# The slots' gates in an expert layer: fp32 products, or float32r products with the gates' high and low parts side by side

## Chip, cores and metric

The kernel runs on one core of one Trainium2 chip. The metric is device microseconds of one execution; lower is better. The profiled execution is one further run, whose trace gives the durations used below.

## What is computed

A model of three blocks is applied to 256 tokens of width 1024. Two blocks each end in a two-level mixture of experts; the third has none. For each token, one of four expert groups is picked, and in it two of four experts; each chosen expert's result is weighted by a gate, and all other gates of the token are zero:

```python
gates = sum(one_hot(flat_idx, 16) * (g_w * e_w)[..., None], axis=1)
for e in range(16):
    hid = silu(xt @ w_gate[e]) * (xt @ w_up[e])
    y = y + gates[:, e:e + 1] * (hid @ w_down[e])
```

All arrays are float32. The change lies in how the kernel brings these gates to the place where the experts use them.

## The kernel before

**Work and staging.** 128 partitions hold 128 tokens each of two token tiles, t = 0 and 1. All large weights come from HBM in pieces of 1 MB, by one queue (SP, line 210), into a ring of buffers; in an expert layer there are 17 of them (12 of the kernel's own, 4 and 1 opened for the layer). A new piece is loaded when the buffer that it needs has been freed, so the loads run ahead of TensorE (PE) by up to the size of the ring. An expert takes six pieces: gate and up weights in four, down weights in two.

**An expert layer** (function moe, called at lines 1192 and 1374) routes first, then runs 16 experts in order. Each expert has 64 slots. Which token sits in which slot is held as a one-hot matrix: places(g) (line 770) builds, for the four experts of group g, the tile oh, with tokens on partitions and 4 x 64 slots along the row, in float32r. VectorE (DVE) writes it. PE uses oh to gather the experts' tokens (line 783) as float32r products: the normalised tokens lie there as a high part th and a low part tl, and each is multiplied by oh.

**Gates.** route_done (lines 745 to 762) works out the gates on DVE and ScalarE (ACT); its last instruction writes the tile gates, 128 x 2 x 16 float32. It runs once a layer. slot_gates(g, oh) then carries them from tokens to slots. Four PE products (two pairs of experts i, two token tiles t) have 128 columns of oh, read as float32, as their stationary operand, and four columns of gates as the moving one, accumulating over t into pg, 128 x 8 in PSUM (line 797). DVE multiplies pg by the mask par, which keeps for each half of the partitions the column of its own expert (line 799, tile gs), and sums along the row into gc (line 800). gc is the scalar by which hidden multiplies an expert's hidden values (line 829).

**Where slot_gates stands.** For group 0 it is issued between the gate and up products of expert 0 (lines 817, 818) and its hidden values; right after route_done was issued. For the other three groups it stands at the end of experts 3, 7 and 11: after the down products (line 843) and after gated (lines 850 to 854, which make the tile Y on DVE and ACT), ahead of the gate and up products of the next expert and of scatter (line 860), which adds Y to the tokens' sums z. That is four calls a layer, eight in all.

**Order of the work.** Up to the zeroing and filling of z (lines 960 to 965) the order on PE, DVE and ACT is as written (manual_schedule with three engines). Afterwards only PE's order is as written; the order on DVE and ACT is set when the program is built, by estimated times. Between two experts stands a branch (line 920, more), for experts with more than 64 tokens; values_load reads the count that it tests. The hidden values are transposed (turn, line 836) behind that branch.

Of the kernel before, what the change touches and what calls it, by code (L numbers as in the profile page):

```python
# [10 lines left out]
F32 = mybir.dt.float32  # L11
F32R = mybir.dt.float32r
# [3 lines left out]
OP = mybir.AluOpType  # L16
AX = mybir.AxisListType
# [3 lines left out]
P = 128  # L21
# [151 lines left out]
def model(ctx: ExitStack, tc: tile.TileContext, A, out, stop=None):  # L173
    nc = tc.nc
    V, S, T, G = nc.vector, nc.scalar, nc.tensor, nc.gpsimd
# [5 lines left out]
    def bank(tag, name, shape=(P, 512), dt=F32):  # L181
        return ps.tile(list(shape), dt, name=name, tag=tag)
# [106 lines left out]
    par = cst.tile([P, 2, 4], F32, name="par")  # L289
# [356 lines left out]
    def moe(l, wr, lb, pl, late):  # L646
        a2, b2 = mod[f"a2_{l}"], mod[f"b2_{l}"]
        with more_ring, tc.tile_pool(name=f"moe{l}", bufs=1, reuse_waits="tile") as mp, \
# [6 lines left out]
            sm = lambda shape, n, dt=F32: mp.tile([P] + shape, dt, name=n)  # L655
# [85 lines left out]
            gc = sm([8], "gc")  # L741
            gates = sm([2, 16], "gates")

            def route_done():
                V.tensor_tensor(eg, lg[:, :, 0:4], gm[:, :, None].to_broadcast([P, 2, 4]), op=OP.subtract)
                S.activation(eg, eg, AF.Exp)
                de = sm([2, 4], "de")
                V.tensor_tensor(de, mm2, m1, op=OP.subtract)
                V.tensor_tensor(de, de, og, op=OP.mult)
                V.tensor_reduce(ew[:, 1], de, axis=AX.X, op=OP.add)  # L750
                S.activation(ew[:, 1], ew[:, 1], AF.Exp)
                V.tensor_reduce(gw, eg, axis=AX.X, op=OP.add)
                V.reciprocal(gw, gw)
                V.tensor_scalar(ew[:, 0], ew[:, 1], 1.0, None, op0=OP.add)
                V.reciprocal(ew[:, 0], ew[:, 0])
                V.tensor_tensor(ew[:, 0], ew[:, 0], gw, op=OP.mult)
                V.tensor_tensor(ew[:, 1], ew[:, 1], ew[:, 0], op=OP.mult)
                wide = lambda v: v[..., None].to_broadcast([P, 2, 4, 4])
                for i, o in enumerate((o1, o2)):
                    V.tensor_tensor(de, og, ew[:, i, :, None].to_broadcast([P, 2, 4]), op=OP.mult)  # L760
                    V.tensor_tensor(o, o, wide(de), op=OP.mult)
                V.tensor_tensor(grid(gates), o1, o2, op=OP.add)

            xi = sm([16], "xi", I32)

            def places(g):

                oh = mw.tile([P, 2, 4, 64], F32R, name="oh", bufs=1)
                for t in range(2):
                    V.tensor_tensor(oh[:, t], iota64[:, None, :].to_broadcast([P, 4, 64]),  # L770
                                    r[:, t, 4 * g:4 * g + 4, None].to_broadcast([P, 4, 64]), op=OP.is_equal)
                return oh
# [18 lines left out]

            def slot_gates(g, oh):

                pg = bank("B", "pg")[:, :8].rearrange("p (i e) -> p i e", i=2)
                for i in range(2):
                    for t in range(2):
                        T.matmul(pg[:, i], oh[:, t, 2 * i:2 * i + 2].bitcast(F32), gates[:, t, 4 * g:4 * g + 4], start=t == 0, stop=t == 1)
                gs = mw.tile([P, 2, 4], F32, name="gs")
                V.tensor_tensor(gs, pg, par, op=OP.mult)
                V.tensor_reduce(gc[:, 2 * g:2 * g + 2], gs, axis=AX.X, op=OP.add)  # L800

            def oht_of(e, off):
                p = bank("B", "oht")[:, :256]
# [134 lines left out]
            oh = places(0)  # L938
# [8 lines left out]
            for k in (0, 4):  # L947
                gather(oh, xg, range(k, k + 4), True)
                some_fill(99 if k else FD)
                warm(W[5 + k // 4])  # L950
            route_done()
            nv = nc.values_load(xi[0:1, 0:1], min_val=0, max_val=3)
            tc.mark_branch_hint_location(f"more{l}_0", hint=nv > 0, engines=[mybir.EngineType.PE])
            w = [take(f"moe{l}", 0, t) for t in range(6)]
            hd0 = half(0, w, xg, 0, lambda: slot_gates(0, oh))
            z = [[bank("C", "z"), bank("C", "z")], [bank("D", "z"), bank("D", "z")]]

# [10 lines left out]
            for e in range(16):  # L968
                more(e, w, nv)
                with ExitStack() as part:  # L970
# [22 lines left out]
                    if e in GA:  # L993

                        ks = GA[e]
                        if ks[0] == 0:
                            oh = places(e // 4 + 1)
# [29 lines left out]
                    if e % 4 == 3:  # L1027
                        xg = xn
                        slot_gates(e // 4 + 1, oh)
# [18 lines left out]
    with tc.tile_pool(name="act0", bufs=1, reuse_waits="tile") as pools["act"], \  # L1048
# [71 lines left out]
        oh = pools["act"].tile([P, KD, NT], F32R, name="xh", tag="xh")  # L1120
# [67 lines left out]
    if stop == "xa0":  # L1188
        for t in range(2):
            nc.sync.dma_start(out[t * P:(t + 1) * P], x[t])  # L1190
        return
    sq = moe(0, *rt, pl, ("ada1", "bsh1_1", "bsc1_1", "n1_1", mod["a1_1"], mod["b1_1"]))
    if stop == "xm0":
        for t in range(2):
# [8 lines left out]
    with tc.tile_pool(name="a1", bufs=1, reuse_waits="tile") as a1, tc.tile_pool(name="act1", bufs=1, reuse_waits="tile") as pools["act"], \  # L1203
# [75 lines left out]
        oh = pools["act"].tile([P, KD, NT], F32R, name="oh", tag="xh")  # L1279
# [89 lines left out]
    if stop == "xa1":  # L1369
        for t in range(2):  # L1370
            nc.sync.dma_start(out[t * P:(t + 1) * P], x[t])
        return
    use_c(1)
    sq = moe(1, *rt, pl, ("ada2", "bsh_2", "bsc_2", "gpre", mod["a_2"], mod["b_2"]))
    if stop == "xm1":
        for t in range(2):
# [5 lines left out]
    with tc.tile_pool(name="b2", bufs=1, reuse_waits="tile") as b2, tc.tile_pool(name="act2", bufs=2, reuse_waits="tile") as pools["act"], tc.tile_pool(name="lk2", bufs=2, reuse_waits="tile") as pools["lk"], \  # L1382
# [207 lines left out]
        oh = pools["act"].tile([P, KD, NT], F32R, name="xh", tag="xh")  # L1590
# [19 lines left out]
        p = [bank("A", "pt0"), bank("A", "pt1")]  # L1610
# [35 lines left out]
```

## Time and profile before

| | |
|---|---|
| median of 3 runs | 1191.7 us (1190.25, 1191.7, 1200.09) |
| profiled execution | 1196.26 us, span 1194.4 us |
| PE busy | 1103.3 us, 92% |
| PE weight loads busy | 787.8 us, 66% |
| DVE busy | 644.3 us, 54% |
| ACT busy | 415.2 us, 35% |
| bytes read from HBM | 350 MB, 294 GB/s over the span |

The span runs from the first to the last instruction of the profiled execution; its time has another 1.9 us around it. PE is the matmul itself, PEld the load of the stationary operand, which may lie beside matmuls. One float32 product appears as two records, two weight loads and two matmuls; a float32r product as one of each. The trace writes float32r operands of a product as f32. Busy times of pipelined matmuls overlap, so a pace is read from the starts of a run of them.

### The profile page before, as it was taken

How to read it: one execution, taken by the hardware profiler on the slowest of the kernel's cores; microseconds unless marked ns; L12 is line 12 of the kernel's file. 1: busy time of each engine (PE TensorE's matmuls, PEld its weight loads, DVE VectorE, ACT ScalarE, POOL GpSimd, SP SyncE). 2: the span in 40 equal slices, each digit the busy share in tenths (PEclk: the TensorE clock that was granted, in tenths of full speed). 3: DMA queues.
4: the chain of work that ended last, by engine and by line, in shares of the span. 5: the costliest groups of instructions: out<-in, count | busy, mean ns of one | idle time of the engine just before them, and what ended most of it. 6: DMA issues, size and time to landing. Idle time of an engine off the chain costs nothing. (4 is left out here: it accounts for less than half of the span.)

```text
span 1194.4 us, 20819 instructions
## 1 busy us (share of the span) xinstructions
PE 1103.3 (92%) x8172; PEld 787.8 (66%) x8172; DVE 644.3 (54%) x1488; ACT 415.2 (35%) x802; POOL 23.1 (2%) x48
## 2 busy tenths in 40 slices
PE   5899998999999989999998998998889999999996
PEld 3786565555555469867654554554478889788995
DVE  4665564333333359887632333332399897667566
ACT  2434432111111154365311211111257546455443
POOL 0000000000000000000000000000012000000000
PEclk9899989999999999999999999999999999999998
DMA  9999868999999987668857999998466445543440
GB/s 381 406 396 418 333 232 340 416 415 416 418 417 418 396 311 291 241 227 324 343 218 281 406 407 393 381 406 317 170 212 217 156 148 181 177 165 140 146 172 36
DMA packets 51064, 354.42 MB, mean 297 GB/s; under 512 B 6160, under 2 KB 6544, under 8 KB 9296
## 3 DMA queue, kind: packets, MB, share of 16 engines
q1 hardware_dynamic: 48544, 344.59, 73.7%
q0 software_dynamic: 2064, 7.08, 1.9%
q8 instruction: 104, 1.70, 0.6%
q14 instruction: 64, 0.52, 0.1%
q10 hardware_dynamic: 288, 0.52, 0.1%
HBM read 350.07 MB, written 1.05 MB: 294 GB/s over the span
## 5 line engine op out<-in xcount | busy, mean ns | idle before, releaser
L818 PE MATMUL gu<-ring,xg 128*64 128x256 f32 x1024 | 240.6, 389 | 2.3 <-issue 2.3
L817 PE MATMUL gu<-ring,xg 128*64 128x256 f32 x1024 | 240.3, 389 | 1.9 <-issue 1.8
L473 PE MATMUL pw<-xh,wh 128*128 128x256 f32 x736 | 211.5, 289 | 7.5 <-ACT wh L456 2.6
L459 DVE TENSOR_TENSOR wl<-ring,wh 128x1024 fp32r<-128x1024 f32 x144 | 175.2, 1221 | 74.3 <-ACT wh L456 70.2
L475 PE MATMUL pw<-xh,wl 128*128 128x256 f32 x736 | 209.2, 285 | 0.8 <-DVE wl L459 0.8
L474 PE MATMUL pw<-xl,wh 128*128 128x256 f32 x736 | 208.6, 284 | 0.0
L817 PEld LDWEIGHTS gu<-ring,xg 128*64 128x64 f32 x1024 | 139.6, 140 | 70.5 <-issue 11.2
L456 ACT ACTIVATE wh<-ring 128x1024 fp32r<-128x1024 f32 x114 | 120.0, 1058 | 152.4 <-PE pw L474 75.6
L473 PEld LDWEIGHTS pw<-xh,wh 128*128 128x128 f32 x736 | 141.3, 193 | 19.1 <-issue 10.0
L818 PEld LDWEIGHTS gu<-ring,xg 128*64 128x64 f32 x1024 | 139.6, 140 | 18.9 <-issue 10.4
L475 PEld LDWEIGHTS pw<-xh,wl 128*128 128x128 f32 x736 | 141.6, 193 | 3.5 <-DVE wl L459 1.9
L474 PEld LDWEIGHTS pw<-xl,wh 128*128 128x128 f32 x736 | 141.7, 193 | 0.9 <-DVE ge L1084 0.4
L843 PE MATMUL y<-ring,ht 128*64 128x512 f32 (+1 forms) x576 | 128.3, 563 | 6.7 <-DVE ht L837 5.0
L829 DVE SCALAR_TENSOR_TENSOR hd<-hs,gc,gu 64x256 f32<-64x256 f32 x64 | 30.7, 480 | 165.8 <-ACT hs L828 165.8
L828 ACT ACTIVATE hs<-gu 64x256 f32<-64x256 f32 x66 | 25.0, 378 | 252.1 <-PE gu L818 252.1
L353 PE MATMUL ada<-ring,zc 128*32 128x256 f32 x960 | 68.9, 393 | 14.0 <-DMA ring<-ada 11.3
L843 PEld LDWEIGHTS y<-ring,ht 128*64 128x64 f32 x576 | 39.4, 137 | 53.6 <-issue 33.8
L853 ACT ACTIVATE Y<-yf 64x512 fp32r<-64x512 f32 (+1 forms) x72 | 42.7, 593 | 91.3 <-DVE yf L850 90.4
L854 DVE TENSOR_TENSOR Y<-yf,Y 64x512 fp32r<-64x512 f32 (+1 forms) x72 | 46.2, 642 | 22.7 <-ACT Y L853 21.3
L490 PE MATMUL pt<-wh,xh 128*128 128x512 f32 x144 | 57.0, 398 | 1.0 <-ACT wh L456 0.4
L492 PE MATMUL pt<-wl,xh 128*128 128x512 f32 x144 | 56.5, 392 | 0.5 <-DVE wl L459 0.5
L491 PE MATMUL pt<-wh,xl 128*128 128x512 f32 x144 | 56.3, 391 | 0.0
(391 smaller groups left out, 1528.0 us busy)
## 6 DMA issues: line engine op xcount, KB each, us to landing
ring<-moe SPq DMA_DIRECT2D x192, 1024.0 KB, 9.5
ring<-ada SPq DMA_DIRECT2D x60, 1024.0 KB, 9.5
ring<-b_z SPq DMA_DIRECT2D x24, 1024.0 KB, 4.8
ring<-b_x SPq DMA_DIRECT2D x12, 1024.0 KB, 5.5
ring<-od_q SPq DMA_DIRECT2D x8, 1024.0 KB, 10.1
ring<-ev_q SPq DMA_DIRECT2D x6, 1024.0 KB, 18.2
ring<-ev_v SPq DMA_DIRECT2D x4, 1024.0 KB, 15.6
ring<-ev_o SPq DMA_DIRECT2D x4, 1024.0 KB, 15.7
```

The source lines that it names most:

```text
L353: T.matmul(p[32 * j:32 * j + 32, :256], zc[:, k, 7 - r:39 - r], w[:, k], start=start and k < 4, stop=stop and k >= 4, skip_group_check=True)
L456: S.activation(h, w, AF.Copy)
L459: V.tensor_tensor(l, w, h.bitcast(F32), op=OP.subtract)
L473: T.matmul(p, hk, xh[:, k], start=k == 0, stop=False)
L474: T.matmul(p, hk, xl[:, k], start=False, stop=False)
L475: T.matmul(p, lk, xh[:, k], start=False, stop=k == KD - 1)
L490: T.matmul(p[t], xh[:, k, n], hk, start=k == 0, stop=False)
L491: T.matmul(p[t], xl[:, k, n], hk, start=False, stop=False)
L492: T.matmul(p[t], xh[:, k, n], lk, start=False, stop=k == KD - 1)
L817: T.matmul(p[gs_], xg[:, k], wg[:, k], start=k == 0, stop=k == KD - 1)
L818: T.matmul(p[us], xg[:, k], wu[:, k], start=k == 0, stop=k == KD - 1)
L843: T.matmul(y[64 * h:64 * h + 64, cs], ht[:, k], wd[:, k % 2, h, cs], start=k == 0 and cs.start == 0, stop=k == 3, skip_group_check=cs != s ...
```

## The change

A tile ghl, 128 x 2 x 2 x 16 in float32r, holds for each token tile the gates rounded to float32r (the high parts) and, beside them, what is left of the float32 value (the low parts). route_done fills it with two more DVE instructions. slot_gates multiplies the same one-hot columns, now as float32r, by eight columns of ghl, four high and four low, so pg and gs have 16 columns in place of 8, and the sum along the row adds high and low parts of the one expert that the mask keeps. more_tokens still reads gates.

```diff
+            ghl = sm([2, 2, 16], "ghl", F32R)
...
                 V.tensor_tensor(grid(gates), o1, o2, op=OP.add)
+                V.tensor_copy(ghl[:, :, 0], gates)
+                V.tensor_tensor(ghl[:, :, 1], gates, ghl[:, :, 0].bitcast(F32), op=OP.subtract)
...
-                pg = bank("B", "pg")[:, :8].rearrange("p (i e) -> p i e", i=2)
+                pg = bank("B", "pg")[:, :16].rearrange("p (i h e) -> p i h e", i=2, h=2)
                 for i in range(2):
                     for t in range(2):
-                        T.matmul(pg[:, i], oh[:, t, 2 * i:2 * i + 2].bitcast(F32), gates[:, t, 4 * g:4 * g + 4], start=t == 0, stop=t == 1)
-                gs = mw.tile([P, 2, 4], F32, name="gs")
-                V.tensor_tensor(gs, pg, par, op=OP.mult)
-                V.tensor_reduce(gc[:, 2 * g:2 * g + 2], gs, axis=AX.X, op=OP.add)
+                        T.matmul(pg[:, i], oh[:, t, 2 * i:2 * i + 2], ghl[:, t, :, 4 * g:4 * g + 4], start=t == 0, stop=t == 1)
+                gs = mw.tile([P, 2, 2, 4], F32, name="gs")
+                V.tensor_tensor(gs, pg, par[:, :, None, :].to_broadcast([P, 2, 2, 4]), op=OP.mult)
+                V.tensor_reduce(gc[:, 2 * g:2 * g + 2], gs.rearrange("p i h e -> p i (h e)"), axis=AX.X, op=OP.add)
```

## Rows read from the trace of the kernel before

**Rows 1.** The page's first part: busy time and share of each engine.
```profile
PE 1103.3 (92%) x8172; PEld 787.8 (66%) x8172; DVE 644.3 (54%) x1488; ACT 415.2 (35%) x802; POOL 23.1 (2%) x48
```
**Rows 2.** Busy by window: PE, PEld, DVE, ACT, POOL, clock, DMA share, GB/s.
```profile
313.00:372.00 59.00, 55.63 (x393) 30.96 (x390) 18.55 (x39) 9.69 (x20) 0.00 (x0) 1.00 1.01 417
```
**Rows 3.** Waits, 195 to 425 us: us in total, times, longest.
```profile
PEld hidT L836 <- PEq L920: 13.0, 15, 1.2
...
PEld pg L797 <- issue: 2.4, 3, 0.8
```
**Rows 4.** Waits of the SP queue alone, 200 to 430 us.
```profile
SPq L210 <- PEq L920: 68.1, 15, 5.8
SPq L210 <- PE y L843: 50.1, 16, 8.0
SPq L210 <- PE gu L818: 48.0, 15, 4.6
```
**Rows 5.** Line 210, 200 to 430 us: issues (first, last start), and landing times.
```profile
L210 SPq DMA_DIRECT2D ring<-moe x77: 327/328/1152, 202.9 to 391.4; - x77
...
DMA to landing us min/median/max: 5.2/11.6/18.8
```
**Rows 6.** Tile pg: matmuls of the whole run, ns min/median/max.
```profile
L797 PE MATMUL pg<-gates,oh x64: 252/253/273, 192.8 to 802.6; 128*128 128x4 f32 x64
```
**Rows 7.** Timeline around the call for group 1, layer 0: start, us, what.
```profile
252.12 1.05 PE L797 MATMUL pg<-gates,oh 128*128 128x4 f32 x8
252.24 0.69 DVE L850 TENSOR_TENSOR yf<-y,g2dup 128x512 f32<-128x512 f32 x1 [1.33 <-PE y L843]
...
253.11 0.43 PE L817 MATMUL gu<-ring,xg 128*64 128x256 f32 x1
...
253.21 0.17 DVE L799 TENSOR_TENSOR gs<-pg,par 128x8 f32<-128x8 f32 x1 [0.28 <-PE pg L797]
...
254.14 1.40 DVE L854 TENSOR_TENSOR Y<-yf,Y 64x512 fp32r<-64x512 f32 x2
...
256.71 1.19 PE L860 MATMUL z<-Y,oht 128*128 128x512 f32 x4
```
**Rows 8.** Timeline around the first call of layer 0 and of layer 1.
```profile
191.78 0.19 DVE L762 TENSOR_TENSOR gates<-o,o 128x32 f32<-128x32 f32 x1
...
192.82 1.05 PE L797 MATMUL pg<-gates,oh 128*128 128x4 f32 x8
...
196.59 0.31 PE L836 MATMUL hidT<-ident,hd 64*128 64x64 f32 x2 [1.84 <-DVEq L920]
...
593.85 0.19 DVE L761 TENSOR_TENSOR o<-o,de 128x32 f32<-128x32 f32 x1
...
594.08 0.19 DVE L762 TENSOR_TENSOR gates<-o,o 128x32 f32<-128x32 f32 x1
...
594.91 1.05 PE L797 MATMUL pg<-gates,oh 128*128 128x4 f32 x8
```
**Rows 9.** Timeline, other one-record products: gather in float32r, rank in bf16.
```profile
185.93 0.63 PE L783 MATMUL gat<-oh,tl 128*128 128x256 f32 x4
...
179.15 0.10 PEld L729 LDWEIGHTS <-tri 128*128 128x128 bf16 x1 [0.41 <-issue]
...
179.25 0.10 PEld L733 LDWEIGHTS <-onesb 128*128 128x128 bf16 x1
```
**Rows 10.** Tile oh: the gather's high-part products of the whole run.
```profile
L783 PE MATMUL gat<-oh,th x128: 274/282/390, 181.2 to 799.6; 128*128 128x256 f32 x128
```
**Rows 11.** Busy by window, PE alone, then all engines; columns as in rows 2.
```profile
194.00:196.00 2.00, 0.75 (x4) 1.00 0.53 209
...
252.00:254.00 2.00, 2.00 (x18) 1.00 1.03 430
...
198.00:200.00 2.00, 2.00 (x12) 1.20 (x10) 0.09 (x1) 0.00 (x0) 0.00 (x0) 0.50 1.00 410
200.00:202.00 2.00, 2.00 (x14) 1.15 (x12) 0.00 (x0) 0.00 (x0) 0.00 (x0) 0.67 0.96 381
```

## The prediction

> **What bounds the kernel now.** I read the page's busy shares first, then the windows of the expert layers, then who waited for whom there, and last the queue that loads the weights. PE is busy 92% of the span and no other engine is over 66% [rows 1]; but shares are averages, and the change touches only the two expert layers. There two things run at their limit at once: in a stretch without a disturbance PE is busy 55.63 of 59 us, while the DMA share is 1.01 at 417 GB/s [rows 2]. Which of the two sets the pace is seen in the waits. The reader is to look for a PE wait that names a DMA: over layer 0's experts there is none. PE's named idle time belongs to the branch between experts (13.0 us in 15 waits) and to "issue" ahead of products like these [rows 3]. From the other side, the queue that loads the pieces waits for PE to free a buffer: three PE releasers alone account for 166 of 230 us [rows 4]. 77 pieces were issued in 188.5 us, one every 2.48 us, so 17 buffers hold some 42 us of PE's work; a piece lands at worst 18.8 us after its issue [rows 5]. So weights lie ready, and PE's own order of work sets the time, the eight calls of slot_gates in it.
>
> **The change part by part.**
>
> *The products.* There are 64 matmul records of slot_gates, eight a call, each 253 ns [rows 6]. In a run they start at a pace: eight take 1.05 us, so (1.05 - 0.253) / 7 = 0.114 us from one to the next [rows 6, 7]. Four float32 products are eight records, because each is carried out twice. A float32r product is one record: the gather's high-part products have 128 [rows 10], which is 2 layers x 4 groups x 8 pieces x 2 token tiles, one each. So a call goes from eight records to four. What pace will the four have? No row shows a float32r product with eight columns. The nearest is the gather, 128 stationary columns too, four products in 0.63 us: (0.63 - 0.282) / 3 = 0.116 us, with 256 moving columns [rows 9, 10]. At the other end are the bf16 products of the rank, five weight loads from 179.15 to 179.25, 0.025 us apart [rows 9]. On the slow side stands the scatter, float32r with 512 columns, four in 1.19 us [rows 7]; at its pace the call would be 0.14 us longer than now. I take 0.114: with four columns the moving side is nothing, the pace of today's records is that of bringing in 128 four-byte columns, and float32r has the same bytes. A call then takes 0.253 + 3 x 0.114 = 0.595 us in place of 1.05, a saving of 0.455 us. Bounds: 7 x 0.114 - 3 x 0.025 = 0.72 us saved at bf16's pace, 0.14 us lost at the scatter's. Doubling the moving columns from four to eight costs nothing that any row could show.
>
> The page "FP8 and Floating Point Precision" of the Trainium skill (TensorE Precision Notes) says that true fp32 takes four passes through the array. If reduced fp32 takes one of the four, three quarters of the pace would go by that rule, an estimate of 0.69 us a call and 5.5 us in all, close to rival B; the two records per product seen here speak for a half.
>
> *The saving on the path, six calls in mid-layer.* At group 1 of layer 0, PE goes from the last gate product straight to the next expert's products at 253.11, 0.06 us before the eight records end [rows 7]. The next expert's weights are there and pg is read by DVE only, so PE moves up by the whole 0.455 us. What is late next? The scatter at 256.71 would come to 256.25; its Y is done by 254.14 + 1.40 = 255.54, so 0.7 us are spare. DVE now waits 0.28 us for pg behind yf [rows 7]; that wait goes, worth nothing. Should the order set at build put gs ahead of yf, Y would come later by about the wait plus 0.3 us, within that margin. The hidden values need gc over 3 us later. Six calls: 2.73 us.
>
> *The two first calls.* Here DVE is next on the path: hidT at 196.59 waits for DVE's arrival at the branch, and DVE's work ahead of it is held up by gs, which waits for pg [rows 8]. An earlier pg moves that whole chain, again 0.455 us. Against it: two DVE instructions stand between gates and the products. Such small 128 x 32 steps follow each other at 0.23 us (593.85 to 594.08). In layer 1 gates starts at 594.08, the copy at 594.31, the difference at 594.54, done 594.73; the products start at 594.91, with 0.18 us to spare. In layer 0: 191.78 + 0.46 + 0.19 = 192.43 against 192.82 [rows 8]. So PE's work on expert 0 hides them. Were that cover gone, as with a 0.3 us longer copy, the two calls would lose some 0.1 us each. The mask product and sum over 16 elements in place of 8 lie between 0.17 us (8 elements) and 0.19 us (32): under 0.02 us each, for both instructions and both layers 0.05 us in all. Queued behind DVE's copy are the mask product, the next one-hot tile and the copies to z; none is due before pg. Two calls: 0.91 - 0.05 = 0.86 us.
>
> No DMA is added or moved; loads follow PE's frees, 0.455 us earlier after each call.
>
> *The sum.* 2.73 + 0.86 = 3.6 us. The profiled execution of 1196.26 us would become 1192.7. That one lies 4.6 us above the median of the runs; the saving is the same there: 1191.7 - 3.6 = 1188.1 us.
>
> **The rivals.**
>
> *A, the loads take it back: no change, 1191.7 us.* With the DMA share at 1.01 [rows 2] an earlier free brings no earlier landing; PE would eat its lead and then wait for weights. For it: in that stretch pieces come no faster than they are used. Against: the 42 us of buffered work less 18.8 us of landing leave more than 20 us, and a layer's four calls use up 1.8. It decides only where the lead is nearly gone.
>
> *B, the load of the weights gets short as well: 1191.7 - 5.8 = 1185.9 us.* If float32r goes in at the pace of the bf16 rank, a call saves 0.72 us. For it: the gather's 0.116 us could be due to its 256 columns, which hide a shorter load. Against: today's fp32 records show 0.114 with no columns to speak of. The page "TensorE: Matmul & The Clock Gate" of the Trainium skill (Weight-path perf modes) says that a fast weight load is on with 128 columns and a type that is not fp32, without a gain for four-byte weights; no run here shows it for float32r.
>
> *C, the change doesn't do what it says: 1191.7 us.* The small float32r products are still carried out twice. Against it: one record per product in the gather. For it: no float32r product with so few columns is in the trace.
>
> *D, slower: the clock.* In layer 0 PE had little to do between the first call and hidT (0.75 of 2 us busy at 194 to 196), and from 198 on the granted clock was 0.50, the lower of its two levels, until it rose again: 2 us and 0.67 x 2 us, about 3.4 us at half speed, 1.7 us lost [rows 11]. If the shortened run of narrow products brought such a drop at each of the six mid-layer calls, it would cost 10.1 us, and 1191.7 - 3.6 + 10.1 = 1198.2 us. It decides from three of the six calls on (5.1 us over 3.6). Against it: PE has no pause there, 252 to 254 is busy throughout at full clock [rows 11], and less narrow work brings the wide work nearer.
>
> **How the numbers follow.** My forecast has 0.70, A 0.11, B 0.09, C 0.05, D 0.05. The predicted time is the forecast's, 1188.1. Range: the products' pace leaves 1185.9 (B) to 1191.7 (A, C; the scatter's pace would give 1192.8). The clock's drops, of 1.7 us each, shift with the time at which work falls, and I allow two either way, 3.4 us; another 1 us for a median of few runs. That gives 1181.5 to 1196. About 1%, 11.9 us, is what a measurement of this kernel can tell from no change. No case of mine reaches it by itself: faster by over 1% needs B and four drops fewer, 0.04; slower by over 1% needs D and several drops more, 0.03; within 1%, 0.93.
>
> **What would show it.** Right: 32 records for the products, one-record form, four in about 0.6 us; the next expert's first product some 0.45 us sooner after the down products; scatter without a new wait on Y; the pair of new DVE steps ended before PE reaches the first call; no PE wait that names a DMA in the expert layers; the same number of clock drops. Wrong: 64 records (C); four records in under 0.4 us (B); a PE wait on the ring (A); clock below 1.00 after groups 1 to 3's calls (D).

## The result: 1.4% slower

The changed kernel takes 1213.28 us (median of 4 runs, 1209.73 to 1215.09), the kernel before, beside it, 1193.38 us: a ratio of 1.0144, with a 95% interval of 1.0112 to 1.0175. The forecast was 3.6 us faster; it came out 20 us slower by the medians, 17 us by the ratio, outside the range. The profiled execution has a span of 1213.0 us against 1194.4.

The products themselves did what was forecast. In the timeline of the changed kernel around the call for group 1 of layer 0 [rows 7]:

```profile
255.97 0.61 PE L801 MATMUL pg<-ghl,oh 128*128 128x8 f32 x4
...
256.51 0.43 PE L821 MATMUL gu<-ring,xg 128*64 128x256 f32 x1
```

Four records take 0.61 us in place of eight in 1.05, and the next expert's products start 0.54 us after the first of them, where it was 0.99: 0.45 us saved. The tile pg has half the records [rows 6]:

```profile
L801 PE MATMUL pg<-ghl,oh x32: 252/253/274, 192.8 to 821.0; 128*128 128x8 f32 x32
```

The two new DVE steps lie where they were put, here ahead of layer 1's first call [rows 8]:

```profile
614.51 0.19 DVE L764 TENSOR_TENSOR gates<-o,o 128x32 f32<-128x32 f32 x1
...
614.74 0.18 DVE L765 CAST ghl<-gates 128x32 fp32r<-128x32 f32 x1
...
614.95 0.19 DVE L766 TENSOR_TENSOR ghl<-gates,ghl 128x32 fp32r<-128x32 f32 x1
...
615.32 0.52 PEld L801 LDWEIGHTS pg<-ghl,oh 128*128 128x128 f32 x4 [0.39 <-DVE ghl L766]
```

The products start 0.81 us after gates, before it was 0.83, so these steps cost nothing, though the wait in front of the products now bears their name. The two first calls gained what was forecast, too: from the start of gates to the first hidT product it was 4.81 us in layer 0 and 4.62 us in layer 1, and is now 4.37 and 4.16.

**Where the time went.** From the first to the last one-hot product of an expert layer (line 805, now 809), layer 0 takes 243.3 us in place of 222.3, layer 1 249.0 in place of 250.6. So the loss lies in layer 0. Its two windows, before and then changed, with the columns of rows 2:

```profile
197.00:419.00 222.00, 208.50 (x1468) 117.04 (x1468) 70.58 (x147) 36.96 (x72) 0.00 (x0) 0.99 1.00 407
```
```profile
197.00:440.00 243.00, 215.71 (x1457) 121.99 (x1456) 70.19 (x146) 36.96 (x72) 0.00 (x0) 0.95 0.94 373
```

PE's idle time grows from 13.5 to 27.3 us. Its busy time grows by 7.2 us although it has less to do, with the granted clock down from 0.99 to 0.95. Together that is the 21 us. The weights came at 373 GB/s in place of 407: they wait for PE, not PE for them. The waits of layer 0 say what PE idles for, in the changed kernel (195 to 430 us) [rows 3]:

```profile
PEld hidT L840 <- PEq L924: 20.1, 15, 5.1
...
PEld gu L821 <- issue: 14.5, 44, 3.0
...
PE gu L821 <- issue: 7.7, 3, 3.7
```

Before, the first of these was 13.0 us, the second, in the same view:

```profile
PEld gu L817 <- issue: 4.5, 18, 0.3
```

The third has no row of that size before. No other engine and no transfer of data is named in these rows. PE waits for its own sequencer (PEq) at the branch, and for "issue", which is time without a releaser in the profile, in the middle of a run of equal products. The largest pause of the first kind stands ahead of expert 8:

```profile
323.97 1.20 PE L864 MATMUL z<-Y,oht 128*128 128x512 f32 x4
...
329.86 0.44 PE L840 MATMUL hidT<-ident,hd 64*128 64x64 f32 x2 [4.69 <-PEq L924]
...
331.27 0.63 PE L821 MATMUL gu<-ring,xg 128*64 128x256 f32 x1
```

The reader is to see two things: 4.7 us without a matmul, and behind it products of 0.63 us that took 0.38 before the pause, at the lower of the clock's two levels (granted clock 0.50 from 331 to 334, 1.00 from 321 to 323). The branch instruction on PE (min/median/max in ns) tells the same. It is one compare and one jump over the more-block, the same for each expert; before, then changed:

```profile
L920 PEldq COMPARE_BRANCH  x34: 89/455/3145, 192.1 to 847.7; - x34
```
```profile
L924 PEldq COMPARE_BRANCH  x34: 89/446/6518, 192.5 to 866.1; - x34
```

The two shortest, 0.09 and 0.20 us, belong to the one more-block that is executed, in layer 1; all others take 0.35 us or more.

### The profile page after: what moved, and what is told of

Same layout as the page of the kernel before. It is cut to its first block, busy times and chain, and to the rows that moved or that the text cites. A ratio compares the mean times of both kernels' runs of the same rounds, so it can differ in the third digit from the quotient of the medians.

```text
span 1213.0 us, 20759 instructions
## 1 busy us (share of the span) xinstructions
PE 1108.7 (91%) x8140; PEld 791.5 (65%) x8140; DVE 644.4 (53%) x1492; ACT 415.3 (34%) x802; POOL 23.3 (2%) x48
## 3 DMA queue, kind: packets, MB, share of 16 engines
HBM read 350.07 MB, written 1.05 MB: 289 GB/s over the span
## 5 line engine op out<-in xcount | busy, mean ns | idle before, releaser
L821 PE MATMUL gu<-ring,xg 128*64 128x256 f32 x1024 | 247.0, 395 | 13.9 <-issue 13.8
L822 PE MATMUL gu<-ring,xg 128*64 128x256 f32 x1024 | 247.2, 396 | 0.9 <-issue 0.9
L821 PEld LDWEIGHTS gu<-ring,xg 128*64 128x64 f32 x1024 | 141.6, 142 | 84.1 <-issue 26.3
L822 PEld LDWEIGHTS gu<-ring,xg 128*64 128x64 f32 x1024 | 141.7, 142 | 16.9 <-issue 8.7
L841 DVE COPY ht<-hidT 128x128 f32<-128x128 f32 x66 | 19.2, 292 | 70.2 <-PE hidT L840 70.2
```

The costliest lines, as they stand in the source:

```text
L821: T.matmul(p[gs_], xg[:, k], wg[:, k], start=k == 0, stop=k == KD - 1)
L822: T.matmul(p[us], xg[:, k], wu[:, k], start=k == 0, stop=k == KD - 1)
```

## The experiments

**Two theories.** *Position:* PE's code is fetched while the kernel runs; a jump to code that isn't there yet makes PE wait. A float32 product was two loads and two matmuls, a float32r product is one of each, so a call has eight instructions fewer, and all code behind it lies elsewhere, eight places earlier with each further call. The order of all instructions on PE, DVE and ACT is otherwise unchanged. *Gates:* the new products or the new DVE steps cost this themselves, by their form or by their place.

**Eight instructions put back, and executed.** In slot_gates, ahead of the products:

```diff
+                for _ in range(4):
+                    T.matmul(pb[:, 32:36], identb, identb[:, 0:4], start=True, stop=True, skip_group_check=True)
```

> The changed kernel, with four tiny bf16 products (128 stationary, 4 moving columns) ahead of the four float32r products in each call, so that TensorE executes 16 instructions a call as before the change (a float32 product was two loads and two matmuls). Position theory (the gain is there, but the eight missing instructions a call move all later code, and the jumps over the more-blocks then meet code that has not been brought in yet): 1187 to 1197 us, ratio to before 0.995 to 1.003, branch times and pauses as before the change. Gates theory (the float32r products or their DVE steps themselves cost): stays at about 1213 us, ratio 1.014.

Measured: 1193.61 us beside 1198.64 for the kernel before, ratio 0.9966 (0.9935 to 0.9996). Four useless products more, and the loss is gone. Layer 0 takes 221.2 us. The gates theory falls: all its instructions are still in this kernel.

**No branches, before and after the change.** The calls of more, the reads of the counts and the hints are taken out of both kernels:

```diff
-                more(e, w, nv)
...
-                        nv = nc.values_load(xi[0:1, e + 1:e + 2], min_val=0, max_val=3)
-                        tc.mark_branch_hint_location(f"more{l}_{e + 1}", hint=nv > 0, engines=[mybir.EngineType.PE])
```

> The kernel before, without the branches between experts: the more-blocks, the reads of the counts and the branch hints are left out, so tokens beyond 64 of an expert (one expert of layer 1) are not computed. Both theories: faster than before, by the 12 us or so of the executed block and by the pauses at the branches, some 25 to 40 us in all, 1150 to 1170 us. It is the base for the next run.

> The changed kernel without the branches, with the same left out as in the run before it. Position theory: with code executed in the order in which it lies there is nothing to miss, so the 3.6 us of the forecast appear: ratio to the no-branch kernel before the change 0.996 to 0.998. Gates theory: the loss stays, 15 to 20 us slower than that kernel.

Measured: 1140.15 and 1136.51 us, in ratios to the kernel before 0.9534 (0.9504 to 0.9563) and 0.9494 (0.9459 to 0.9529). The first is lower than expected (1150 to 1170 us); the second is 0.997 of the first, as expected. The difference of 3.6 us is the forecast's sum, but the two intervals overlap; the trace is sharper, and the saving can be read off one expert. Here is the one-hot product of experts 3 and 4 of layer 0, between which the call for group 1 lies, without branches, first before and then after the change:

```profile
237.28 0.29 PE L805 MATMUL oht<-identb,rb 128*128 128x128 bf16 x2
...
253.03 0.28 PE L805 MATMUL oht<-identb,rb 128*128 128x128 bf16 x2
```
```profile
237.91 0.29 PE L809 MATMUL oht<-identb,rb 128*128 128x128 bf16 x2
...
253.20 0.29 PE L809 MATMUL oht<-identb,rb 128*128 128x128 bf16 x2
```

15.75 us become 15.29, 0.46 less; the other two experts with a call in mid-layer take 0.45 us less each, and experts without one take the same in both. A layer's experts take 1.4 us less by it, in both layers, and from gates to the first hidT product it is 0.39 us less (3.08 and 2.69): 2 x 1.4 + 2 x 0.39 = 3.6 us. Where PE's code runs straight on, the change is worth what its products save; from 200 to 400 us PE has no pause of over 0.6 us in either of the two kernels.

**The kernel before, its code moved.** First with executed products ahead of layer 0's experts:

```diff
+            if l == 0:
+                pad = bank("A", "pad")
+                for _ in range(64):
+                    T.matmul(pad[:, 0:4], identb, identb[:, 0:4], start=True, stop=True, skip_group_check=True)
```

> The kernel before, with 64 tiny bf16 products (128 instructions) added once, on TensorE ahead of layer 0's experts, in the pause of the routing; nothing else changes. The products themselves cost 64 x 0.025 = 1.6 us, up to 3 us at the lower clock. Position theory: the time moves by clearly more than that, most likely up, to 1200 to 1220 us, with pauses and branch times at other experts than before. Gates theory: 1193 to 1197 us, pauses where they were.

Measured: 1216.25 us, ratio 1.0173 (1.0127 to 1.0218). Layer 0's experts, all behind the added products, take 230.3 us in place of 222.3, layer 1's 256.3 in place of 250.6. This kernel has none of the change and loses as much.

Executed products also shift the moments at which everything falls. So the same products were put inside the more-block of expert 0 of layer 0, where they are jumped over, once 64 and once 128:

```diff
+                if b == 1 and l == 0 and e == 0:
+                    for _ in range(64):
+                        T.matmul(pqb[:, 32:36], identb, identb[:, 0:4], start=True, stop=True, skip_group_check=True)
```

> The kernel before, with 64 tiny bf16 products (128 instructions) inside the more-block of expert 0 of layer 0, which is jumped over and not executed. What is executed is the kernel before, instruction for instruction; only the code behind lies 128 instructions further on. Position theory: the time moves clearly, as in the run with 64 executed products (1.017): 1205 to 1220 us, ratio over 1.008. Rival (the executed instructions and the moments at which they fall make the pauses): no change, ratio 0.997 to 1.003.

> The same with 128 tiny products (256 instructions) in that block, not executed. If code is brought in by blocks of 256 instructions, as the bytes per packet of the instruction queue suggest (1.70 MB in 104 packets, 16 KB each, at 64 bytes an instruction), a shift by one whole block changes nothing: ratio 0.997 to 1.003, pauses and branch times at the same experts as before. If there is no such period: another time again, 1200 to 1220 us.

Measured: 1213.78 us with 64, ratio 1.0137 (1.0100 to 1.0173); 1195.17 us with 128, ratio 0.9985 (0.9964 to 1.0005). Both execute exactly what the kernel before executes. Code moved by 128 instructions costs 1.4%, moved by 256 nothing. Three kinds of PE's pauses in the two, columns as in rows 3, first 64 and then 128:

```profile
PE gu L818 <- issue: 9.1, 5, 2.7
...
PE gu L817 <- issue: 6.3, 4, 2.8
PE hidT L836 <- PEq L924: 6.2, 12, 1.5
```
```profile
PE hidT L836 <- PEq L924: 7.5, 13, 1.7
...
PE gu L818 <- issue: 2.2, 1, 2.2
...
PE gu L817 <- issue: 2.1, 2, 1.8
```

With 64 the loss is not at the jump but some products behind it: 15.4 us of "issue" within the gate and up products, 4.3 us with 128. The period of 256 was expected from the profile page's row of the instruction queue, 1.70 MB in 104 packets, 16 KB each:

```profile
q8 instruction: 104, 1.70, 0.6%
```

The page "Runtime: NRT & Kernel Launch" of the Trainium skill (Instruction fetch mechanics) says the same, blocks of 16 KiB or 256 instructions, and that a taken branch to a block that isn't there has to wait for its fetch. The runs agree with the 256, which makes 64 bytes an instruction.

**The changed kernel's places, with the old products.** 248 instructions, 256 less 8, not executed, in the more-blocks behind each call:

```diff
+                if b == 1 and e % 4 == 0:
+                    for _ in range(124):
+                        T.matmul(pqb[:, 32:36], identb, identb[:, 0:4], start=True, stop=True, skip_group_check=True)
```

> The kernel before, its fp32 products kept, with 124 tiny products (248 instructions) in the more-blocks of experts 0, 4, 8 and 12 of both layers, jumped over and not executed. 248 is 256 less 8, so behind each of these blocks the code lies, within its block of 256, where the changed kernel has it, which lacks 8 instructions a call. Position theory: the changed kernel's loss without its products, 1.4% and the 3.6 us of the gain on top: 1212 to 1220 us, ratio 1.012 to 1.020, with the long branch times and pauses at the experts of the changed kernel (over 4 us ahead of expert 8 of layer 0, a pause in expert 14). If the float32r products had a part in the loss: less than 1.010.

Measured: 1218.85 us, ratio 1.0163 (1.0110 to 1.0216). Layer 0 takes 244.1 us, layer 1 249.1, against 243.3 and 249.0 in the changed kernel. The pause in the second half of expert 13 (experts count from 0; the expectation called it the fourteenth), in this kernel and then in the changed one:

```profile
417.26 0.59 PE L817 MATMUL gu<-ring,xg 128*64 128x256 f32 x1 [3.75 <-issue]
```
```profile
410.42 0.59 PE L821 MATMUL gu<-ring,xg 128*64 128x256 f32 x1 [3.72 <-issue]
```

The same product, the same length. At expert 8 the expectation missed in size: the branch took 3.8 us, not 6.5, and the pause was 1.9 us, while one in expert 3 was 3.4 us where the changed kernel has 1.4. The places of the pauses are set by the code, their lengths vary.

**Why the fetch is late.** Half of each piece of layer 0's weights is not loaded:

```diff
-            nc.sync.dma_start(w, flat(plan[j][1]))
+            if plan[j][0][0] == "moe0" and plan[j][0][1] > 0:
+                nc.sync.dma_start(w[:, 0:1024], flat(plan[j][1])[:, 0:1024])
+                G.memset(w[:, 1024:2048], 0.0)
+            else:
+                nc.sync.dma_start(w, flat(plan[j][1]))
```

> The changed kernel, with only half of each piece of weights loaded for experts 1 to 15 of layer 0; the other half is set to zero by GpSimd. It leaves half of those weights out, and tells whether the loads' traffic makes the code come late. If traffic does: layer 0's experts, from the first one-hot product to the last, shrink from 243 us towards 222 us or less, branch times over 1.5 us are gone there, and the whole comes to 1185 to 1195 us. If bringing in code takes that long by itself: 240 us or more, the same pauses at the same experts.

> The kernel before with half of each piece loaded for experts 1 to 15 of layer 0, the other half zero, as in the changed kernel's run of that kind (which leaves half of those weights out). With the code's delay gone on both sides the products alone should differ: from the first one-hot product to the last, layer 0 takes the changed kernel's 220.2 us and 3 calls x 0.455 us more, 221.6 us, give or take 1. If the position still counts at half the traffic: off by several us, either way.

Measured, one execution each: 1192.14 and 1194.8 us. The changed kernel's layer 0 falls from 243.3 to 220.2 us; that of the kernel before, from 222.3 to 220.6. PE executes the same code at the same places; only the traffic is less:

```profile
197.00:418.00 221.00, 207.29 (x1458) 117.46 (x1458) 70.99 (x148) 36.95 (x72) 71.86 (x79) 0.99 0.65 224
```

At a DMA share of 0.65 in place of 0.94 the pauses of over 1 us between experts 2 and 13, six in the changed kernel, are gone. So the code comes late because its fetch meets the weight loads, and whether that makes PE wait depends on where it lies. The two kernels differ by 0.4 us in layer 0 and not by the 1.4 of three calls; the changed one still has one branch of 2.3 us there, which the expectation took to be gone, and one execution can't tell such a size.

The kept traces show the fetches themselves, as packets of 16 KB on the instruction queue q8 (104 in the kernel before, 63 without the branches). Here are the changed kernel's branch ahead of expert 8, then what the DMA queues moved from 322.9 to 327.0 us, and from 327.0 to 328.2 (packets, MB, share of the 16 engines; q1 carries the weights):

```profile
L924 PEldq COMPARE_BRANCH  x1: 6518/6518/6518, 322.9 to 322.9; - x1
```
```profile
q1 hardware_dynamic: 242, 1.75, 100.8%
```
```profile
q1 hardware_dynamic: 56, 0.42, 84.9%
q8 instruction: 1, 0.02, 5.8%
```

For four microseconds of the branch the weights have the DMA engines to themselves; then one packet of code comes, lands at 328.17, and the branch ends 1.3 us later. It is so throughout: in the ten kernels with branches, each of the 118 PE branches of over 1 us ends 1.3 to 1.7 us after such a packet has landed, and each of the 36 pauses of over 1 us ahead of a gate or up product ends 1.2 to 1.7 us after one. In layer 0 of the changed kernel the next packet starts 3.7 us after the start of a short branch (under 0.7 us; median of 9), with half the loads 1.1 us (median of 12); the packet itself takes 1.0 us in both.

**A version that beats both.** The changed kernel, its eight instructions put back where they are not executed:

```diff
+                if b == 1 and e % 4 == 0:
+                    for _ in range(4):
+                        T.matmul(pqb[:, 32:36], identb, identb[:, 0:4], start=True, stop=True, skip_group_check=True)
```

> The changed kernel with the eight missing instructions of a call put back as four tiny products in the more-blocks of experts 0, 4, 8 and 12 of both layers, where they are jumped over and not executed. Position theory: pauses as in the kernel before, and the whole gain of the four float32r products: 3.6 us faster than before, ratio 0.994 to 0.999, slightly better than with four executed products. Gates theory: 1.014.

Measured: 1193.77 us beside 1196.83 for the kernel before, ratio 0.9961 (0.9936 to 0.9985), the one of all kernels that do the whole work with the lowest ratio. Whether it is better than the one that executes the four products (0.9966) can't be told.

## Why the prediction was wrong

1. *What bounds the kernel.* Right that PE's own order sets the time and that no load of weights is waited for; nothing of that kind is in the changed trace either. The 13.0 us of waits at the branch [rows 3] were mostly the branch's price, as taken: with half the loads 12.3 us of them are left. But the same kernel's branches spread from 0.35 to 3.1 us, and that this was code coming late was not asked; in its layer 0 it cost little, 222.3 us against 220.6 with half the loads.
2. *The products.* Right: 32 records, 0.61 us a call against 0.595 forecast, 0.45 to 0.46 us saved. The pace with eight columns is (0.61 - 0.253) / 3 = 0.119 us, against 0.114 taken. B and C fell.
3. *The two first calls, the cover of the DVE steps, the scatter, the mask.* Right: 0.44 and 0.46 us for the first calls, 0.90 us against 0.86 forecast, with nothing to pay.
4. *The step that failed* is "PE moves up by the whole 0.455 us. What is late next?" It was asked of Y, gc, the weights and the clock, and not of PE's code. "From eight records to four" was counted as time saved, and not as eight instructions fewer in a stream that is fetched by blocks while it jumps over a more-block more than 30 times. In its place the runs showed 21 us lost in layer 0, 13.8 us of it more idle time of PE, most of it pauses that end behind a late packet of code, and 7.2 us more busy time, with the clock at its lower level for longer.
5. *The rivals.* A fell. D named a part of the price, the lower clock after a time with little to do, but the wrong cause: past the drop at expert 0 that both kernels have, the granted clock of layer 0 was 0.50 for 3.4 us twice (from 228.4 and 296.7) and for 6.8 us twice (from 327.4 and 409.3), each time during or within 2 us of a pause for code of 1.7 us or more, and not behind the narrow products. No rival had the cause, and with no case over 1198.2 us the range ended at 1196 and slower by over 1% had 0.03.
6. *The sum* of 3.6 us was right wherever code was out of the question: 3.6 us without branches, and 3.1 and 5.0 us by the medians (4.7 and 4.1 by the ratios, whose intervals reach from 0.5 to 7.8 us) where the old places were restored.

Two kinds of fetch are late, by the packets that end the waits: that of the jump's target, where the branch itself is long, and that of a block behind it, where PE stops within a run of products. Open is a rule that tells from the places of the code which fetch will be late; layer 1 of the changed kernel has its code moved as well and lost nothing (249.0 us against 250.6). The branch hint's part was not tried.

## What to carry to other kernels

In a kernel with branches, a change of the number of instructions on an engine moves all of its code behind, and that alone can cost more than the change saves, here some 20 us against 3.6. If a trace shows new pauses that name only the engine's own sequencer or "issue", restore the old places with instructions inside a block that is jumped over, and measure again before judging the change. A comparison without the branches shows what the change itself is worth.

## What was not expected of the hardware

- Code that is never executed, 128 instructions in a jumped-over block, cost 1.4% of the time of a kernel whose executed instructions were unchanged; 256 cost nothing.
- The jump over a more-block took PE from 0.35 to 6.5 us in one kernel, beside weight loads at a DMA share of 0.94. The long ones end 1.3 to 1.7 us after a 16 KB packet of code has landed.
- Eight columns in a float32r product cost hardly more than four in a float32 one: the pace was 0.119 us a record, before 0.114, so four products took 0.61 us in place of 1.05.
